# Grouped-query attention: VectorE empties two PSUM banks per instruction, chains of eight, last store on another queue

## The chip, the cores and the metric

The kernel runs on one core of a Trainium2 chip. The metric is device time in microseconds (us) of one execution; a median over runs is quoted. Ratios are computed as the mean time of one kernel's fast runs over that of the other's fast runs of the same rounds, with a 95% interval, so they are not quite the ratio of the medians. In the profiles PE is TensorE (PEld its weight loads), ACT is ScalarE, DVE is VectorE, POOL is GpSimd and SP is SyncE. Profiles are of single executions; the profiled span is about 1.7 us shorter than the device time.

## The reference, cut to what matters

```python
batch, n_q_heads, n_kv_heads, seq, head_dim = (8, 8, 2, 1024, 64)
scores = scale * np.matmul(q_group, k_group.transpose(0, 1, 3, 2))
attn = np.exp(scores - scores.max(-1, keepdims=True))
output = np.matmul(attn / attn.sum(-1, keepdims=True), v_group)
```

There are 64 heads. The kernel cuts each into two jobs of 512 queries, and each job into eight **cells** of 128 keys x 512 queries: 128 jobs, 1024 cells.

## The kernel before

PE computes the scores of a cell into one PSUM bank. Most cells go to ScalarE, which exponentiates two banks with one instruction. The others go to VectorE: it writes the scores as the bits of a power of two (evacuation), and a chain of four operations over a group of cells corrects them (named and, line, prod and add; line runs on POOL). PE then multiplies the result with the values ("output matmuls", 4 per cell), and VectorE normalises each job. A planner with a cost table decides at build time which cell goes where and in which order every engine runs; engines execute that order.

```python
A_CELLS, D_BANKS, O_BANKS = (2, 2), 2, 2     # ScalarE: 2 slots of 2 banks; VectorE: 2 single banks
GROUP, PARTS = 10, 2                         # cells per chain
...
    QK, PV, P1, NORM = 0.216, 0.1225, 0.603, 0.555
    EXP = (0.05, 0.4268)                     # planned cost of an exponential: fixed, per cell
...
    def exps(n, cells):                      # ScalarE
        act = nc.scalar.activation(
            out=pt[:, 0:m], in_=psum.pop(("A", n))[:, 0:m], func=AF.Exp, scale=scale
        )
...
    def exp_bits(cell, n, g, slot):          # VectorE, one bank
        nc.vector.tensor_scalar(
            out=groups[g][:, slot], in0=psum.pop(cell),
            scalar1=bits_scale, scalar2=bits_bias, op0=ALU.mult, op1=ALU.add,
        )
...
    def put_out(b, h, sides):
        nc.sync.dma_start(out=..., in_=stage[(b, h)][:, :, sides])
```

(cut at the marks and inside the calls)

The softmax here doesn't subtract the row's maximum and nothing guards it: scores larger than these inputs give would overflow.

## Time and profile before

| | before |
|---|---|
| device time, median of the first 3 runs | 385.65 us (385.5 to 385.9) |
| exponentials on ScalarE (2 cells each) | 404 |
| cells on VectorE | 216 |
| first exponential starts, last one ends | 7.40, 379.44 us |
| last normalisation ends, span ends | 380.59, 384.03 us |

The page's busy lines, its rows and the stages are shown in the prediction. One more view matters, and the prediction did not read it rightly: ScalarE's timeline in two nested windows (start us, length us, engine, line, operation, count).

```profile
157.58 1.94 ACT L477 ACTIVATE p_ring<-aps 128x1024 bf16<-128x1024 f32 x2
157.58 6.52 ACT L477 ACTIVATE p_ring<-aps 128x1024 bf16<-128x1024 f32 x7
```

A merged line ends where its last instruction ends. The second exponential of this stretch ends at 157.58 + 1.94 = 159.52, the seventh at 164.10: five intervals between **ends** take 4.58 us, 0.916 each. The trace's **starts** of the same instructions (158.50 to 163.015) take 4.517 us, 0.903 each. The recorded duration makes up the difference: 1.018, 1.032, 1.045, 1.058, 1.072, 1.085, some 13 ns more each time.

### The profile page before, as it was taken

How to read it: one execution, taken by the hardware profiler on the slowest of the kernel's cores; microseconds unless marked ns; L12 is line 12 of the kernel's file. 1: busy time of each engine (PE TensorE's matmuls, PEld its weight loads, DVE VectorE, ACT ScalarE, POOL GpSimd, SP SyncE). 2: the span in 40 equal slices, each digit the busy share in tenths (PEclk: the TensorE clock that was granted, in tenths of full speed). 3: DMA queues.
4: the chain of work that ended last, by engine and by line, in shares of the span. 5: the costliest groups of instructions: out<-in, count | busy, mean ns of one | idle time of the engine just before them, and what ended most of it. 6: DMA issues, size and time to landing. Idle time of an engine off the chain costs nothing.

```text
span 384.0 us, 12026 instructions
## 1 busy us (share of the span) xinstructions
PE 365.6 (95%) x5172; PEld 233.6 (61%) x5172; DVE 353.8 (92%) x548; ACT 374.6 (98%) x409; POOL 174.4 (45%) x147
## 2 busy tenths in 40 slices
PE   8879898999999999999999999999999999998995
PEld 7425464666666666666666666666666666564664
DVE  4779998999999999999999999999999999989982
ACT  5999999999999999999999999999999999999995
POOL 5584535718244371563718245271643627040420
PEclk9999999999999999999999999999999999999999
DMA  8988988697756848585676759468675765711213
GB/s 137 135 152 135 130 154 124 129 147 140 113 109 132 140 103 139 101 156 103 139 131 120 130 106 152 96 126 137 105 124 123 138 102 119 126 56 29 57 56 84
DMA packets 102485, 45.48 MB, mean 118 GB/s; under 512 B 63792, under 2 KB 100976, under 8 KB 101184
## 3 DMA queue, kind: packets, MB, share of 16 engines
q1 hardware_dynamic: 82096, 31.21, 36.1%
q0 software_dynamic: 19712, 13.18, 32.3%
q8 instruction: 40, 0.66, 0.7%
q10 hardware_dynamic: 624, 0.33, 0.3%
q14 instruction: 13, 0.11, 0.1%
HBM read 25.17 MB, written 27.00 MB: 136 GB/s over the span
## 4 chain that ended last, share of the span: by engine, by line
ACT 86%; PE 10%; DVE 2%; issue 1%
ACT p_ring L477 86%; PE aps L466 4%; PE ops L538 4%; PE ops L409 1%; PE dps L466 1%; DVE pd L527 1%; DVE ost L554 0%; DVE y L525 0%; DVE z L512 0%; DVE rec L551 0%; PE dps L382 0%; PE dps L428 0%; PE ops L428 0%; PE aps L382 0%; DVE blank L288 0%
## 5 line engine op out<-in xcount | busy, mean ns | idle before, releaser
L477 ACT ACTIVATE p_ring<-aps 128x1024 bf16<-128x1024 f32 x404 | 371.8, 1067 | 1.4 <-PE aps L466 1.2
L466 PE MATMUL aps<-qT,kset 128*128 128x512 bf16 x808 | 239.9, 378 | 13.0 <-ACT p_ring L477 12.4
L538 PEld LDWEIGHTS <-p_ring 128*128 128x128 bf16 x3232 | 140.1, 98 | 64.0
L538 PE MATMUL ops<-vset,p_ring 128*128 128x65 bf16 x3232 | 154.6, 194 | 0.0
L491 DVE TENSOR_SCALAR pd<-dps 128x512 uint16<-128x512 f32 x216 | 138.6, 683 | 7.0 <-PE dps L466 6.7
L516 POOL TENSOR_SCALAR y<-z 128x5120 f16<-128x5120 uint16 (+1 forms) x22 | 96.4, 4383 | 70.0 <-DVE rec L551 48.7
L466 PEld LDWEIGHTS <-kset 128*128 128x128 bf16 x1024 | 79.7, 97 | 56.4 <-issue 25.8
L323 POOL DMA_DIRECT2D scr_q<-in_q_dram x63 | 39.1, 621 | 83.5 <-PE dps L466 44.3
L466 PE MATMUL dps<-qT,kset 128*128 128x512 bf16 x216 | 76.4, 379 | 0.0
L525 DVE TENSOR_TENSOR y<-z,y 128x5120 f16<-128x5120 uint16 (+1 forms) x22 | 61.0, 2772 | 1.1 <-POOL y L516 1.1
L527 DVE TENSOR_TENSOR pd<-pd,y 128x5120 uint16<-128x5120 uint16 (+1 forms) x22 | 60.9, 2769 | 0.1
L554 DVE TENSOR_TENSOR ost<-ops,rec 128x256 f32<-128x256 f32 x128 | 54.3, 425 | 4.4
L538 PEld LDWEIGHTS <-pd 128*128 128x128 bf16 x864 | 42.8, 98 | 24.7 <-DVE ost L554 2.2
L538 PE MATMUL ops<-vset,pd 128*128 128x65 bf16 x864 | 52.2, 194 | 0.3
L512 DVE TENSOR_SCALAR z<-pd 128x5120 uint16<-128x5120 uint16 (+1 forms) x22 | 32.3, 1467 | 0.5
L551 DVE RECIPROCAL rec<-ops 128x4 f32<-128x4 f32 x128 | 22.6, 176 | 9.6 <-PE ops L538 8.2
L323 POOL DMA_DIRECT2D scr_k<-in_k_dram x15 | 9.8, 656 | 39.9 <-PE aps L466 33.0
L356 POOL DMA_DIRECT2D vset<-in_v_dram x32 | 24.9, 784 | 0.0
L409 PE MATMUL ops<-blank 128*128 128x128 bf16 x40 | 5.3, 313 | 1.1 <-DVE blank L288 1.1
L409 PEld LDWEIGHTS <-blank 128*128 128x128 bf16 x40 | 4.4, 149 | 1.1 <-DVE blank L288 1.1
L363 POOL DMA_DIRECT2D kset<-kset x6 | 4.1, 684 | 0.0
L420 ACT ACT_TABLE_LOAD x1 | 1.3, 1283 | 1.8 <-issue 1.8
(23 smaller groups left out, 10.2 us busy)
## 6 DMA issues: line engine op xcount, KB each, us to landing
out_dram<-ost SPq DMA_DIRECT2D x63, 256.0 KB, 2.9
scr_q<-in_q_dram POOLq DMA_DIRECT2D x63, 128.0 KB, 3.5
kset<-kT SPq DMA_DIRECT2D x60, 64.0 KB, 3.1
vset<-in_v_dram POOLq DMA_DIRECT2D x32, 64.0 KB, 3.9
scr_k<-in_k_dram POOLq DMA_DIRECT2D x15, 128.0 KB, 3.7
qT<-scr_q SPq DMA_TRANSPOSE x63, 3.5
kset<-kset POOLq DMA_DIRECT2D x6, 128.0 KB, 4.3
fq<-in_q_dram ACTq DMA_DIRECT2D x2, 128.0 KB, 3.3
```

What stands on the lines that cost most here:

```text
L323: dma = nc.gpsimd.dma_start(out=scr.rearrange("(p f) -> p f", f=1024), in_=src.rearrange("(p s) d -> p (s d)", s=1024 // D),)
L356: nc.gpsimd.dma_start(out=vsets[b % 2][:, g, two * NHC : (two + 1) * NHC, 0:D], in_=v[b, g].rearrange("(c p two) d -> two p c d", p=128, t ...
L466: last_score[0] = nc.tensor.matmul(dst, lhsT=ksets[b % 2][:, h // HPG, side, c * 128 : (c + 1) * 128], rhs=qT[(b, h)], start=True, stop=Tr ...
L477: act = nc.scalar.activation(out=pt[:, 0:m], in_=psum.pop(("A", n))[:, 0:m], func=AF.Exp, scale=scale)
L491: nc.vector.tensor_scalar(out=groups[g][:, slot], in0=psum.pop(cell), scalar1=bits_scale, scalar2=bits_bias, op0=ALU.mult, op1=ALU.add,)
L512: eng.tensor_scalar(out=z, in0=pd, scalar1=0x7F, scalar2=None, op0=ALU.bitwise_and)
L516: eng.tensor_scalar(out=y, in0=z, scalar1=CURVE_A / 128.0, scalar2=CURVE_B, op0=ALU.mult, op1=ALU.add,)
L525: eng.tensor_tensor(out=y, in0=z, in1=y, op=ALU.mult)
L527: eng.tensor_tensor(out=pd, in0=pd, in1=y, op=ALU.add)
L538: nc.tensor.matmul(ops_of[s][:, qs, :], lhsT=p_of[cell][:, qs * 128 : (qs + 1) * 128], rhs=vsets[b % 2][:, h // HPG, c, :], start=opens an ...
L551: nc.vector.reciprocal(out=rec, in_=o[:, :, D])
L554: nc.vector.tensor_tensor(out=stage[(b, h)][:, :, side, :], in0=o[:, :, 0:D], in1=rec.unsqueeze(2).to_broadcast([128, NQS, D]), op=ALU.mult,)
```

## The change

The intent: cheaper evacuations (one fixed cost for two banks), so that VectorE has slack; PSUM regrouped into three two-bank slots, two for ScalarE and one for VectorE; short chains at the start and at the end, where a late chain can't hide; the last store on a queue of its own.

```diff
-A_CELLS, D_BANKS, O_BANKS = (2, 2), 2, 2
-GROUP, PARTS = 10, 2
+SLOTS, A_SLOTS, D_SLOTS, O_BANKS = 3, (0, 1), (2,), 2
+GROUP, PARTS = 8, 2
...
-    LIVE_A, LIVE_D, PENDING, PER_JOB, LEAD, RAMP, AHEAD, FIRST_PV = 28, 5, 16, 2, 6, 6, 0.0, 2.0
-    AHEAD_D, EXTRA, LAST = 0, 0, 6
+    LIVE_A, LIVE_D, PENDING, PER_JOB, LEAD, RAMP, AHEAD, FIRST_PV = 28, 5, 12, 2, 4, 6, 0.06, 2.0
+    AHEAD_D = 0.03
+    FIRST_SIZES, FIRST_JOBS, FIRST_MORE = (2, 4, 6), 4, 2
+    LAST_SIZE, LAST_GROUPS, LAST_JOBS, LAST_MORE = 4, 8, 4, 0
...
-            out=groups[g][:, slot],
-            in0=psum.pop(cell),
+            out=groups[g][:, first : first + len(cells)],
+            in0=psum.pop(("D", slot))[:, 0 : len(cells)],
...
+                queue = nc.scalar if op[2] == len(jobs) - 1 else nc.sync
```

(cut: the planner's bookkeeping for pairs of cells, and the names of the PSUM pools)

More of the change, by code (lines that the diff above doesn't have):

```diff
@@ L26, in make_plan @@
 def make_plan(nj, nkc):
-    QK, PV, P1, NORM = 0.216, 0.1225, 0.603, 0.555
-    EXP = (0.05, 0.4268)
+    QK, PV, NORM = 0.216, 0.1225, 0.555
+    EXP, P1 = (0.05, 0.4268), (0.07, 0.533)
     FOUR, TWO, POOL_ONE = (0.09, 0.133), (0.05, 0.27), (0.25, 0.43)
@@ L44, in make_plan @@
     pe = act = dve = pool = two_end = 0.0
-    a_free, bank, obank_free = [0.0] * len(A_CELLS), [0.0] * D_BANKS, [0.0] * O_BANKS
+    free, obank_free = [0.0] * SLOTS, [0.0] * O_BANKS
     todo = [list(range(nkc)) for _ in range(nj)]
@@ L49, in make_plan @@
     open_jobs, next_job, rem, obank = [], 0, {}, {}
-    open_a = None
+    open_a = open_d = None
     ready, home, uses = {}, {}, {}
@@ L61, in loaded, with first_free, per_job, size @@
         return FIRST_LOAD + EACH_LOAD * (h - 1 if h < 4 else h)
-    def first_free(slots):
-        return min(range(len(slots)), key=lambda s: slots[s])
+    def first_free(times, among):
+        return min(among, key=lambda s: times[s])
+    def per_job(j):
+        if j < FIRST_JOBS:
+            return PER_JOB + FIRST_MORE
+        return PER_JOB + LAST_MORE * (j >= nj - LAST_JOBS)
+    def size(g):
+        if g < len(FIRST_SIZES):
+            return FIRST_SIZES[g]
+        return LAST_SIZE if job_d >= nj - LAST_GROUPS else GROUP
     while normed < nj:
@@ L73, in make_plan @@
         while job_d < nj and (
-            taken[job_d] >= PER_JOB + EXTRA * (job_d >= nj - LAST)
-            or not todo[job_d]
+            taken[job_d] >= per_job(job_d)
+            or len(todo[job_d]) < 2
         ):
@@ L82, in make_plan @@
             elif live["A"] < LIVE_A:
-                t = max(pe, min(a_free), loaded(job_a))
+                t = max(pe, min(free[s] for s in A_SLOTS), loaded(job_a))
             if t < INF:
                 best = min(best or (INF,), (t - AHEAD, 1, "qk", 0, t))
-        if job_d < nj and job_d <= job_a + lead + 1 and pending < PENDING:
+        if open_d is not None:
+            t = max(pe, open_d["t"])
+            best = min(best or (INF,), (t - AHEAD_D, 2, "qk", 1, t))
+        elif job_d < nj and job_d <= job_a + lead + 1 and pending < PENDING:
             if cur or live["D"] < LIVE_D:
-                t = max(pe, min(bank), loaded(job_d))
+                t = max(pe, min(free[s] for s in D_SLOTS), loaded(job_d))
                 if t < INF:
@@ L110, in make_plan @@
             best = min(best or (INF,), (at, 2 + i, "chain", i))
-        if cur and job_d >= nj and not p1q:
+        if cur and job_d >= nj and not p1q and open_d is None:
             best = min(best or (INF,), (dve, 9, "flush", 0))
@@ L116, in make_plan @@
             pe = t + QK
-            j = job_d if arg else job_a
-            cell = j * nkc + todo[j].pop(0)
             if not arg:
+                cell = job_a * nkc + todo[job_a].pop(0)
                 if open_a is None:
-                    slot = first_free(a_free)
+                    slot = first_free(free, A_SLOTS)
                     a_id += 1
                     live["A"] += 1
-                    open_a = {"slot": slot, "t": a_free[slot], "cells": []}
-                    a_free[slot] = INF
+                    open_a = {"slot": slot, "t": free[slot], "cells": []}
+                    free[slot] = INF
                 o = open_a
@@ L129, in make_plan @@
                 home[cell] = ("A", a_id)
-                if len(o["cells"]) == A_CELLS[o["slot"]] or not any(todo[job_a:]):
+                if len(o["cells"]) == 2 or not any(todo[job_a:]):
                     act = max(act, pe + FROM_PE)
@@ L133, in make_plan @@
                     act += EXP[0] + EXP[1] * len(o["cells"])
-                    a_free[o["slot"]] = act + FROM_ACT
+                    free[o["slot"]] = act + FROM_ACT
                     uses[("A", a_id)] = len(o["cells"])
@@ L139, in make_plan @@
             else:
-                taken[j] += 1
-                k = first_free(bank)
-                bank[k] = INF
-                pending += 1
-                ops.append((t, "qk", cell, "D", k, 0, 0))
-                p1q.append((pe + FROM_PE, cell, k))
+                if open_d is None:
+                    slot = first_free(free, D_SLOTS)
+                    open_d = {"slot": slot, "t": free[slot], "n": 0}
+                    open_d["cells"] = [job_d * nkc + todo[job_d].pop(0) for _ in range(2)]
+                    free[slot] = INF
+                    taken[job_d] += 2
+                    pending += 2
+                o = open_d
+                cell = o["cells"][o["n"]]
+                ops.append((t, "qk", cell, "D", cell, o["slot"], o["n"]))
+                o["n"] += 1
+                if o["n"] == 2:
+                    p1q.append((pe + FROM_PE, tuple(o["cells"]), o["slot"]))
+                    open_d = None
         elif kind == "open":
-            o = first_free(obank_free)
+            o = first_free(obank_free, range(O_BANKS))
             obank[arg] = o
@@ L174, in make_plan @@
         elif kind == "p1":
-            _, cell, k = p1q.pop(0)
+            _, cells, slot = p1q.pop(0)
             if not cur:
@@ L178, in make_plan @@
                 live["D"] += 1
-            ops.append((t, "p1", cell, k, d_id, len(cur)))
-            dve = t + P1
-            bank[k] = dve + FROM_DVE
-            cur.append(cell)
-            home[cell] = ("D", d_id)
-            if len(cur) == GROUP:
+            ops.append((t, "p1", cells, slot, d_id, len(cur)))
+            dve = t + P1[0] + P1[1] * len(cells)
+            free[slot] = dve + FROM_DVE
+            for x in cells:
+                cur.append(x)
+                home[x] = ("D", d_id)
+            if len(cur) >= size(d_id):
                 chainq.append((dve, d_id, cur, 0))
@@ L282, in psum_pools @@
         ]
-    apools, dbanks, obanks = psum_pools("aps", 2), psum_pools("dps", 2), psum_pools("ops", 2)
+    slots, obanks = psum_pools("sps", SLOTS), psum_pools("ops", O_BANKS)
     p_ring = const_pool.tile([128, P_TILES, 2, QBS], BF16)
@@ L372, in first_loads @@
         hk = first_pool.tile([128, NHC, 3, D], BF16, name="hk")
-        tk = [
-            dbanks[0].tile([128, HALF], BF16, name="dps0"),
-            apools[1].tile([128, HALF], BF16, name="aps1"),
+        spare = [
+            slots[n].tile([128, 2, 2 * QBS], BF16, name=f"sps{n}")[:, 0, :HALF]
+            for n in range(SLOTS)
         ]
+        tk = [spare[2], spare[1]]
         lo, hi = slice(0, D), slice(D, 2 * D)
@@ L412, in first_loads @@
         hq = first_pool.tile([128, NHC, 2 * D], BF16, name="hq")
-        tq = [
-            dbanks[1].tile([128, HALF], BF16, name="dps1"),
-            obanks[0].tile([128, HALF], BF16, name="ops0"),
-        ]
+        tq = [spare[0], obanks[0].tile([128, HALF], BF16, name="ops0")]
         qT[(0, 0)] = qT_pool.tile([128, HALF], BF16, name="qT")
@@ L459, in score @@
         c = cell % NKC
+        if col == 0:
+            psum[kind, slot] = slots[slot].tile([128, 2, QBS], FP32, name=f"sps{slot}")
+        dst = psum[kind, slot][:, col, :]
         if kind == "A":
-            if col == 0:
-                psum[("A", n)] = apools[slot].tile([128, 2, QBS], FP32, name=f"aps{slot}")
-            dst = psum[("A", n)][:, col, :]
-        else:
-            dst = psum[cell] = dbanks[n].tile([128, QBS], FP32, name=f"dps{n}")
+            psum["exp", n] = psum[kind, slot]
         last_score[0] = nc.tensor.matmul(
@@ L477, in exps @@
         act = nc.scalar.activation(
-            out=pt[:, 0:m], in_=psum.pop(("A", n))[:, 0:m], func=AF.Exp, scale=scale
+            out=pt[:, 0:m], in_=psum.pop(("exp", n))[:, 0:m], func=AF.Exp, scale=scale
         )
@@ L486, in exps, with exp_bits @@
             p_of[cell] = pt[:, col, :]
-    def exp_bits(cell, n, g, slot):
-        if slot == 0:
+    def exp_bits(cells, slot, g, first):
+        if first == 0:
             groups[g] = pd_pool.tile([128, GROUP, QBS], U16, name="pd")
         nc.vector.tensor_scalar(
-            out=groups[g][:, slot],
-            in0=psum.pop(cell),
+            out=groups[g][:, first : first + len(cells)],
+            in0=psum.pop(("D", slot))[:, 0 : len(cells)],
             scalar1=bits_scale,
@@ L498, in exp_bits @@
         )
-        p_of[cell] = groups[g][:, slot].bitcast(BF16)
+        for n, cell in enumerate(cells):
+            p_of[cell] = groups[g][:, first + n].bitcast(BF16)
     def exp_curve(g, m, step):
@@ L559, in normalise, with put_out @@
         )
-    def put_out(b, h, sides):
+    def put_out(b, h, sides, queue):
         rows = "(s p two) d -> p s two d"
-        nc.sync.dma_start(
+        queue.dma_start(
             out=out[b, h].rearrange(rows, p=128, two=2)[:, :, sides],
@@ L576 @@
             if op[2] >= len(jobs) - 2:
-                at(op[0] + 0.01, put_out, b, h, slice(side, side + 1))
+                queue = nc.scalar if op[2] == len(jobs) - 1 else nc.sync
+                at(op[0] + 0.01, put_out, b, h, slice(side, side + 1), queue)
             elif ended.setdefault(op[2] // 2, op[2]) != op[2]:
-                at(op[0] + 1.5, put_out, b, h, slice(0, 2))
+                at(op[0] + 1.5, put_out, b, h, slice(0, 2), nc.sync)
         at(op[0], run[op[1]], *op[2:])
```

## The prediction

> **What bounds the kernel now.** I read the page first, then windows, then the chain of waits and PE's timeline near the end. The page's part 1, its chain by engine, and its rows (line, engine, operation, shapes, count | busy us, mean ns | idle before, releaser):
>
> ```profile
> PE 365.6 (95%) x5172; PEld 233.6 (61%) x5172; DVE 353.8 (92%) x548; ACT 374.6 (98%) x409; POOL 174.4 (45%) x147
> ACT 86%; PE 10%; DVE 2%; issue 1%
> L477 ACT ACTIVATE p_ring<-aps 128x1024 bf16<-128x1024 f32 x404 | 371.8, 1067 | 1.4 <-PE aps L466 1.2
> L466 PE MATMUL aps<-qT,kset 128*128 128x512 bf16 x808 | 239.9, 378 | 13.0 <-ACT p_ring L477 12.4
> L491 DVE TENSOR_SCALAR pd<-dps 128x512 uint16<-128x512 f32 x216 | 138.6, 683 | 7.0 <-PE dps L466 6.7
> ```
>
> ScalarE is busy 98% and carries 86% of the chain. Its 404 exponentials of two cells each do 808 of the 1024 score cells; VectorE does the other 216, one cell (one PSUM bank) at a time. Per stage (columns: stretch, length, then busy time of PE, PEld, DVE, ACT, POOL, then granted clock, DMA share, GB/s):
>
> ```profile
> 0.00:10.00 10.00, 8.69 (x72) 6.98 (x73) 4.61 (x13) 5.32 (x8) 5.12 (x15) 1.00 0.77 131
> 60.00:340.00 280.00, 273.69 (x3979) 176.35 (x3975) 273.17 (x420) 279.95 (x306) 129.47 (x103) 1.00 0.71 123
> 340.00:380.00 40.00, 38.07 (x618) 25.29 (x616) 32.79 (x53) 39.34 (x43) 10.98 (x3) 1.00 0.17 48
> ```
>
> In the long middle ScalarE never shows a gap, VectorE is busy 97.6% (273.17 of 280) and PE nearly as much. But "busy" hides small waits on ScalarE: one exponential is recorded as 1.067 us, yet the next starts before its end. The start times in the trace tell the rest: 403 intervals from 7.40 to 378.35 us, shortest 0.903 us, 193 of them under 0.905, mean 0.9205. The excess over 403 x 0.903 = 363.9 is **7.0 us**. In 123 intervals the exponential starts within 45 ns of the modelled end of the second score matmul that feeds it: these PE released, and they hold 5.0 of the 7.0 us. PE's timeline shows why (start, us, engine, line, operation):
>
> ```profile
> 374.00 0.59 PE L466 MATMUL aps<-qT,kset 128*128 128x512 bf16 x2
> 374.44 0.65 PE L538 MATMUL ops<-vset,p_ring 128*128 128x65 bf16 x16
> 374.93 0.59 PE L466 MATMUL aps<-qT,kset 128*128 128x512 bf16 x2
> ```
>
> From one pair of scores for ScalarE to the next, PE spends 0.93 us when 16 output matmuls (4 cells) stand between; that is more than 0.903. The chain of waits splits this step (start, us, what):
>
> ```profile
> 374.17 0.43 PE aps L466 x2
> 374.60 0.49 PE ops L538 x16
> ```
>
> So ScalarE is the bound, and PE's in-order program adds to it whenever one step carries more than 0.903 us of work. Only two PSUM slots feed ScalarE, so PE cannot run ahead to hide it.
>
> **What the Trainium skill says.** "Perfetto Trace Analysis", section "Identifying the Most-Contended Engine", takes occupancy as the measure for ScalarE and VectorE; the 98% agrees, with the correction above that a 98% engine still loses 7 us to late inputs. "VectorE: DVE Perf Modes", section on the TRN2 errata, gives a PSUM to SBUF operation 120 + FD cycles at 0.96 GHz: 658 ns for 512 elements, where the trace has 683. For 1024 it gives 1.19 us; adding 512 elements at 1.04 ns to the traced 683 gives 1.22. "DMA: Bandwidth & Descriptors", section "Issuing engines are not separate DMA queues", says that issuing from another engine saves only the sequencer's time to issue; see the last store below.
>
> **The change part by part.**
>
> *One VectorE instruction for two banks.* In the instruction order of the two built programs 216 evacuations of 512 become 107 of 1024. Three of the old ones in a row take 1.94 us merged, so they follow each other at about (1.94 - 0.68) / 2 = 0.63, at best 0.60 us (two take 1.28). New: estimated 1.22 - 0.08 of overlap = 1.13 us. 216 x 0.60 = 129.6; 107 x 1.13 = 120.9: VectorE saves 8.7 us.
>
> *Chains.* 22 chains (21 of ten cells, one of six) become 30 (23 of eight, two of six, four of four, one of two). From the two forms of each row (5120 and 3072 elements: 1491 and 954 ns, 2820 and 1759, 2817 and 1749) the constant part of an operation is about 0.15 us recorded. Three VectorE operations x 8 more chains x at most 0.15 = +3.6 us; two cells fewer give back 1.3. VectorE ends with some 6.4 us less, near 347 us. POOL's line gets 8 more instructions of a constant of some 0.2 us; at 45% that costs nothing. Since VectorE is off the chain, its saving is worth nothing by itself.
>
> *Cells do not move.* VectorE's share goes from 216 to 214, so ScalarE does 405 exponentials, not 404: **+0.90 us** on the bound.
>
> *PE's order.* The planner is changed (score pairs for VectorE stand together, ScalarE's pairs get 0.06 us of precedence). I counted in the built order what stands between one ScalarE pair and the next. Pair 0.43, VectorE score 0.215, output matmuls 0.03 each:
>
> - 16 outputs: 0.92, over by 0.018: 131 steps before, 177 after
> - one VectorE score and 12 outputs: 1.015, over by 0.11: 26 before, 8 after
> - two and 4: 0.98, over by 0.08: 33 before, 15 after
> - two and 8: over by 0.20: 2 before, none after
> - 20 outputs: over by 0.14: 4 before, none after
>
> Sums: before 2.4 + 2.9 + 2.6 + 0.4 + 0.6 = 8.9 us, after 3.2 + 0.9 + 1.2 = 5.3 us. Light steps in between absorb part of it: of the 8.9 the trace shows 5.0 (0.56). With the same share the new order costs 3.0 us: **-2.0 us**. The gain is that a lone VectorE score with 8 outputs (92 steps) or 12 gives way to whole pairs with none (10 to 73 steps, 0.86 us, which fits).
>
> *Ends.* The first chain is two cells, and the last ones four, so outputs at the ends wait less for VectorE. The first exponential still waits for the same loads, at 7.40 us: nothing. After the last exponential (ends 379.44) the old kernel needs 1.15 us for the last outputs and the normalisation and 3.4 us for the last store and the end: that stays. The issue of the last store was not held up on its old queue: VectorE ends at 380.59, the issue starts at 380.62. It landed 2.5 us later, behind a 256 KB store issued 0.6 us ahead. In the new order the last two normalisations stand further apart, so the last store shares the DMA engines less: about **-0.3 us**, not because of the queue.
>
> Sum: +0.90 - 2.0 - 0.3 = -1.4 us, 384.2. The share of 0.56 is probably lower with many small overruns of 0.018 and few large ones, because a light step absorbs a small one whole; I lower the value to **383.9 us**.
>
> **Rivals.**
>
> 1. *The single VectorE slot stalls PE.* Before, two banks were refilled one at a time; now both belong to one instruction, and PE can't put in a new pair until it is read. A cycle takes some 0.6 (two scores) + 1.2 + waits of 0.1 = 1.9 us; 107 pairs in 350 us come every 3.3 us, so on average it fits, but a chain operation of eight cells takes 8/10 of 2.8 = 2.2 us, and a pair that comes just before it would hold the slot for over 4 us. PE is in order: a wait there delays ScalarE's next pair directly. For it: nothing on PE waits for VectorE before (0.0 idle at its VectorE scores), so there is no measure. Against: VectorE gets slack, 97.6% to some 95%, and the planner places a pair only when it expects the slot to be free. If every tenth pair stalled by 0.4 us: +4 us, 387.5.
> 2. *Nothing but the extra exponential.* If the waits are a matter of how tightly two slots can turn round, not of PE's order, the 7.0 us stay and the time is 385.65 + 0.9 - 0.3 = 386.2. Against it: intervals of 0.92 us (130 of them) and of 0.98 to 1.01 are just what the step sums above give.
> 3. *VectorE was the true limit, and its saving counts.* At 97.6% it paces the output banks and chains. Then the remaining 2 us of excess vanish as well, and the time is near 382. Against: only 2.2 us of weight-load idle is put down to VectorE's normalisation, 1.9 to its chains.
>
> **Range and chances.** With all 7.0 us of excess gone the time would be 385.65 + 0.9 - 7.0 - 0.3 = 379.25, 1.7% under the old: over 2% faster is out of reach unless the lead-in shrinks. Rival 1 has to cost over 9 us for 2% slower. Range 381.9 to 386.2. Faster 0.01, within 2% 0.96, slower 0.03.
>
> **What would show it.** Right: 405 exponentials; evacuations near 1.2 us; VectorE busy near 347 us; VectorE's share of the middle near 95%; mean exponential interval 0.914 to 0.917; no PE row that waits for VectorE over 1 us in total; last store lands 2.0 to 2.3 us after its issue. Wrong: PE scores waiting for VectorE's evacuation by several us (rival 1), an unchanged mean interval of 0.920 (rival 2), or a first exponential later than 7.4 us because the start now uses ScalarE's first slot for a transpose.

## The result, and the profile after

Over 6 runs each, the changed kernel took 384.98 us (384.9 to 385.48), the kernel before 385.77: ratio **0.9984** (0.9971 to 0.9997). In a later set of rounds it was 385.11 against 385.61, 0.9989 (0.9977 to 1.0001). So it is some 0.1 to 0.2% faster, 0.4 to 0.6 us by these ratios (the second interval just takes in 1), where I had predicted 1.75 us (383.9).

The page after, part 1, the chain by engine, and the rows that answer to those shown before. The trace of this execution lacks 92 matmul records (5080 of 5172), so PE's busy times are a little low:

```profile
PE 364.8 (95%) x5080; PEld 235.4 (61%) x5172; DVE 349.3 (91%) x463; ACT 374.4 (98%) x410; POOL 174.1 (45%) x155
...
ACT 91%; PE 5%; DVE 2%; POOL 1%; issue 0%
...
L497 ACT ACTIVATE p_ring<-sps 128x1024 bf16<-128x1024 f32 x405 | 371.7, 1111 | 1.2 <-PE sps L486 1.1
L486 PE MATMUL sps<-qT,kset 128*128 128x512 bf16 x932 | 262.1, 378 | 8.7 <-ACT p_ring L497 6.3
...
L511 DVE TENSOR_SCALAR pd<-sps 128x1024 uint16<-128x1024 f32 x107 | 130.7, 1221 | 11.9 <-PE sps L486 10.7
```

VectorE works less and ScalarE's share of the chain grew from 86% to 91%. The tell-tale is the mean duration of an exponential: 1111 ns, up from 1067, with no more time in total. The stages after:

```profile
0.00:10.00 10.00, 8.56 (x72) 6.86 (x74) 4.54 (x12) 5.76 (x9) 5.67 (x16) 1.00 0.80 137
...
60.00:340.00 280.00, 272.26 (x3874) 176.28 (x3944) 265.82 (x346) 279.71 (x306) 130.89 (x104) 1.00 0.70 121
340.00:380.00 40.00, 37.65 (x584) 25.31 (x591) 34.05 (x53) 39.09 (x43) 8.78 (x4) 1.00 0.21 58
```

VectorE fell from 97.6% to 94.9% of the middle, as expected, and ScalarE did the same 306 exponentials in the same 280 us as before. The chain of waits (the profile's walk back from the instruction that ended last; not to be confused with VectorE's chains) shows the pace: it names ScalarE for stretches of 26 exponentials (start, us, what). Before:

```profile
152.93 23.86 ACT p_ring L477 x26
176.86 23.80 ACT p_ring L477 x26
```

After:

```profile
151.98 23.78 ACT p_ring L497 x26
175.81 23.85 ACT p_ring L497 x26
```

From one stretch to the next it is 23.93 us before and 23.83 after: 0.9204 and 0.9165 us per exponential. PE's lateness did fall, but there were only 0.004 us per exponential to win here.

From here on I use ends of exponentials. In every profile the median interval between ends is 0.916 to 0.917 us; I call **excess** the time from the first to the last end beyond 0.9165 us per interval.

| profile | exponentials | first start | first to last end | excess | intervals over 0.93 | last end to last normalisation | last store, issue to landing |
|---|---|---|---|---|---|---|---|
| before | 404 | 7.40 | 371.01 | 1.66 | 25 | 1.16 | 2.50 |
| after | 405 | 6.96 | 371.10 | 0.84 | 4 | 1.15 | 2.01 |

(landing: when SP's wait for the store ends)

The profiled spans differ by 0.83 us (384.03, 383.21): start -0.44, one exponential +0.92, excess -0.82, last store -0.50, rest +0.01. The start turned out to be chance (below), so what the change brings is about -0.4 us.

### The profile page after: what moved, and what is told of

Same layout as the page of the kernel before. It is cut to its first block, busy times and chain, and to the rows that moved or that the text cites. A ratio compares the mean times of both kernels' runs of the same rounds, so it can differ in the third digit from the quotient of the medians.

```text
span 383.2 us, 11861 instructions
## 1 busy us (share of the span) xinstructions
PE 364.8 (95%) x5080; PEld 235.4 (61%) x5172; DVE 349.3 (91%) x463; ACT 374.4 (98%) x410; POOL 174.1 (45%) x155
## 4 chain that ended last, share of the span: by engine, by line
ACT 91%; PE 5%; DVE 2%; POOL 1%; issue 0%
ACT p_ring L497 91%; PE sps L486 2%; PE ops L433 1%; PE ops L559 1%; POOL y L537 1%; DVE y L546 1%; DVE pd L548 1%; POOL scr_q L346 0%; DVE ost L575 0%; PE sps L406 0%; DVE rec L572 0%; PE ops L449 0%; PE sps L449 0%; POOL vset L379 0%; DVE blank L311 0%
## 5 line engine op out<-in xcount | busy, mean ns | idle before, releaser
L497 ACT ACTIVATE p_ring<-sps 128x1024 bf16<-128x1024 f32 x405 | 371.7, 1111 | 1.2 <-PE sps L486 1.1
L486 PE MATMUL sps<-qT,kset 128*128 128x512 bf16 x932 | 262.1, 378 | 8.7 <-ACT p_ring L497 6.3
L559 PEld LDWEIGHTS <-p_ring 128*128 128x128 bf16 x3240 | 133.7, 97 | 57.0 <-ACT p_ring L497 0.8
L559 PE MATMUL ops<-vset,p_ring 128*128 128x65 bf16 x3240 | 145.9, 194 | 4.1 <-ACT p_ring L497 0.5
L511 DVE TENSOR_SCALAR pd<-sps 128x1024 uint16<-128x1024 f32 x107 | 130.7, 1221 | 11.9 <-PE sps L486 10.7
L537 POOL TENSOR_SCALAR y<-z 128x4096 f16<-128x4096 uint16 (+3 forms) x30 | 97.4, 3248 | 49.2 <-DVE z L533 48.9
L546 DVE TENSOR_TENSOR y<-z,y 128x4096 f16<-128x4096 uint16 (+3 forms) x30 | 61.7, 2056 | 2.8 <-POOL y L537 2.2
L548 DVE TENSOR_TENSOR pd<-pd,y 128x4096 uint16<-128x4096 uint16 (+3 forms) x30 | 61.6, 2054 | 0.3
L559 PE MATMUL ops<-vset,pd 128*128 128x65 bf16 x856 | 40.4, 194 | 1.0 <-DVE pd L548 0.5
L533 DVE TENSOR_SCALAR z<-pd 128x4096 uint16<-128x4096 uint16 (+3 forms) x30 | 33.2, 1109 | 0.8
```

The costliest lines, as they stand in the source:

```text
L486: last_score[0] = nc.tensor.matmul(dst, lhsT=ksets[b % 2][:, h // HPG, side, c * 128 : (c + 1) * 128], rhs=qT[(b, h)], start=True, stop=Tr ...
L497: act = nc.scalar.activation(out=pt[:, 0:m], in_=psum.pop(("exp", n))[:, 0:m], func=AF.Exp, scale=scale)
L511: nc.vector.tensor_scalar(out=groups[g][:, first : first + len(cells)], in0=psum.pop(("D", slot))[:, 0 : len(cells)], scalar1=bits_scale, ...
L533: eng.tensor_scalar(out=z, in0=pd, scalar1=0x7F, scalar2=None, op0=ALU.bitwise_and)
L537: eng.tensor_scalar(out=y, in0=z, scalar1=CURVE_A / 128.0, scalar2=CURVE_B, op0=ALU.mult, op1=ALU.add,)
L546: eng.tensor_tensor(out=y, in0=z, in1=y, op=ALU.mult)
```

## The experiments

"Theory" is that ScalarE's own pace is 0.9165 us and that the time is the number of exponentials at that pace, plus a small excess, plus the two ends.

**1. PE with slack.** Some output steps left out of the kernel before, with a wrong result (the matmul count falls from 5172 to 3640):

```diff
+        if c % 2 and not opens and not closes:
+            p_of.pop(cell)
+            return
```

> The kernel before with about three of eight output steps left out (wrong result on purpose), so that PE has slack and cannot be late for ScalarE. Theory (ScalarE's own pace is 0.9165 us per exponential, measured from end to end; start-to-start intervals of 0.903 only mean that an instruction is recorded earlier and longer): intervals between ends settle at 0.916 to 0.917, the recorded duration saturates near 1.15 us, first to last end takes 403 x 0.9165 = 369.4 us instead of 371.0, and the time falls by about 1.6 us, to some 384.1. Rival (my prediction: pace 0.903, the rest is PE): starts follow at 0.903, first to last start takes 364 us, the time falls by 5 to 7 us, to 379 to 381.

Measured: 384.07 us, ratio 0.996 (0.9947 to 0.9974). Relieved of 30% of its matmuls, PE lets ScalarE run no faster than this (chain of waits):

```profile
152.65 23.79 ACT p_ring L477 x26
176.48 23.79 ACT p_ring L477 x26
```

23.83 us per 26, 0.9165 each, again. The recorded durations climb to 1.15 us and stop there (median 1.130), and starts are then 0.917 apart too. The rival, on which the prediction stood, is refuted: a start that follows 0.903 us after the one before is not a pace that ScalarE can keep. After a late start the durations fall back (to 1.02 to 1.09) and climb again, and while they climb the starts are closer than the ends. A further rival is that the turn-round of the two slots sets this pace: in this run PE's scores began within 60 ns of the end of the exponential two before in 354 of 402 cases. But 169 exponentials began over 60 ns after the modelled end of their scores, so that PE and the slot no longer held them, and their ends too followed 0.917 us after the one before. And 187 exponentials began within 45 ns of their scores, more than the 123 of the kernel before, although PE had slack: that sign does not tell that PE is late. Of the 25 intervals over 0.93 us, 5 remain. First to last end took 370.8 us, not 369.4, because one early interval lost 1.11 us; the waits name its cause:

```profile
PE dps L466 <- DMA kset<-kset: 1.2, 1, 1.2
```

This execution began at 6.55 us instead of 7.40, and PE then waited for a copy of keys: an early start was given back. It is therefore partly luck that the time met the theory's 384.1: against the profile before, the start came 0.86 us earlier and the last store landed 0.29 us sooner, which the wait of 1.11 us nearly cancels.

**2 and 3. The queue of the last store.** The changed kernel with it back on SP's queue, and the kernel before with it on ScalarE's:

```diff
-                queue = nc.scalar if op[2] == len(jobs) - 1 else nc.sync
+                queue = nc.sync
```
```diff
-        nc.sync.dma_start(
+        (queue or nc.sync).dma_start(
...
+                   nc.scalar if op[2] == len(jobs) - 1 else nc.sync)
```

> The changed kernel with the very last store back on SP's queue. Theory (the gain at the end, 0.50 us between issue and landing, comes from the distance to the store before it, not from the queue): the last store still lands about 2.0 us after its issue, and the time stays within 0.1 us of the changed kernel's 384.98. Rival (the queue gives it): the store lands after about 2.5 us and the time is 0.4 to 0.5 us longer, 385.4.

> The kernel before with only its very last store moved to ScalarE's queue. Theory (distance counts, not queue): the store still lands about 2.5 us after its issue because a 256 KB store was issued 0.6 us ahead of it, time within 0.1 us of before, 385.7. Rival (the queue gives it): landing in 2.0 us, time 385.2.

Measured: 385.37 us (0.9990, interval 0.9976 to 1.0004) and 385.37 us (0.9998, 0.9985 to 1.001). The times alone do not tell the theories apart, as 0.4 us lies within both intervals. The traces do: the last store landed 1.98 us after its issue in the first, 2.50 us in the second, each as in the kernel with the same plan (2.01 and 2.50) and not as in the kernel with the same queue. In the plan before, a 256 KB store was issued 0.6 us ahead of the last one; in the plan after, 1.9 us ahead. Profiles of later experiments lie between, each with a 256 KB store ahead: 2.21 us for 0.88 us ahead, 2.16 for 0.93, 2.11 for 0.99. The distance counts. The change of queue brought nothing that these runs show.

**4. One bank per instruction in the new plan.** Same slots, same order, two instructions for each pair:

```diff
-        nc.vector.tensor_scalar(
-            out=groups[g][:, first : first + len(cells)],
-            in0=psum.pop(("D", slot))[:, 0 : len(cells)],
+        src = psum.pop(("D", slot))
+        for n in range(len(cells)):
+            nc.vector.tensor_scalar(
+                out=groups[g][:, first + n],
+                in0=src[:, n],
```

> The changed kernel, same plan and slots, but each evacuation of two banks split again into two VectorE instructions of 512. Theory (VectorE is off the path, its 8 us saved buy nothing by themselves): VectorE's busy time rises by some 7 us to 356, ScalarE's ends still follow at 0.9165, time within 0.5 us of 384.98. Rival (the merged instruction itself brings the gain, because the single slot comes free sooner): PE waits for the slot, ScalarE's excess over 0.9165 per exponential grows from 0.8 us to several, time 386 or more.

Measured: 385.97 us, 1.0009 (0.9995 to 1.0023), 1.0 us above the changed kernel's 384.98 (of another round; 0.6 above experiment 2 of the same round): my theory, that VectorE's saving buys nothing, missed, and the rival came nearer. VectorE was busy 354.5 us. The excess was 2.50 us, nearly all of it in 16 intervals; 0.62 of it is an early wait for the copy of keys as in experiment 1 (this execution began at 6.49 us), the remaining 1.9 compare with 0.84. The largest interval after that, 0.48 us near 252 us, is PE's output matmuls waiting for the last operation of a chain (chain of waits):

```profile
249.24 2.21 DVE pd L550
251.45 0.05 issue
251.50 0.30 PE ops L561 x4
...
252.26 1.94 ACT p_ring L497 x2
```

The scores for ScalarE stand behind the delayed outputs in PE's order. But the changed kernel loses 0.39 us at the same exponential, by the same wait:

```profile
248.48 2.21 DVE pd L548
...
250.73 0.30 PE ops L559 x4
```

So this chain makes 0.08 us of the difference. Most of the rest is the single slot. One case (timeline):

```profile
185.39 1.28 DVE L513 TENSOR_SCALAR pd<-sps 128x512 uint16<-128x512 f32 x2
...
186.21 0.53 PE L561 MATMUL ops<-vset,p_ring 128*128 128x65 bf16 x12
...
186.72 1.02 PE L486 MATMUL sps<-qT,kset 128*128 128x512 bf16 x4
```

The twelve outputs follow each other 0.03 us apart, so PE could begin VectorE's next pair of scores at 186.58. It begins at 186.72, 53 ns after the second evacuation has ended, and ScalarE's pair stands behind it. Counted in this way from the trace and the built order, 31 pairs of VectorE's scores waited for the slot, 2.85 us of PE's time in all, and 13 of the 16 late intervals, with 1.10 us, follow such a pair within 1.3 us. In the changed kernel it is 8 pairs, 0.58 us, and 2 of its 4 late intervals, with 0.14 us. The lists of waits do not show this: an output matmul is recorded as 0.19 us, so a short wait leaves no idle time between records. So the merged instruction is worth some 0.6 to 1 us in this plan, and mainly because the single slot comes free sooner, as the rival had it. Whether through the evacuation itself (1.22 us against 1.28) or because VectorE, with less to do, comes to it sooner was not separated.

**5. The changed kernel again**, as the yardstick for the next runs.

> The changed kernel once more, as the yardstick of this round. Theory: 405 exponentials, first to last end 371.1 us with 4 intervals over 0.93 us, last store landing in 2.0 us; the first exponential starts anywhere from 6.5 to 7.5 us, by when PE's clock comes up in that execution, so its start says nothing about the change. Time 384.8 to 385.4.

Measured: 385.11 us, ratio 0.9989; 371.10 us from first to last end, excess 0.83, 4 intervals over 0.93, landing 2.01 us: all as in the first profile. The first exponential began at 7.26 us instead of 6.96.

**6. Without the precedence for ScalarE's score pairs.**

```diff
-... FIRST_PV = 28, 5, 12, 2, 4, 6, 0.06, 2.0
-    AHEAD_D = 0.03
+... FIRST_PV = 28, 5, 12, 2, 4, 6, 0.0, 2.0
+    AHEAD_D = 0.0
```

> The changed kernel with the planner's precedence for ScalarE's score pairs (0.06 and 0.03 us) set to zero. Its plan has 404 exponentials, one fewer. Theory (ScalarE's pace 0.9165 plus what PE is late): the missing exponential gives -0.92 us, and if the precedence is what keeps PE on time, the excess over 0.9165 grows from 0.8 to 2 us or more and takes that back; at least ten intervals over 0.93 us. Rival (the two-bank slots alone keep PE on time): excess stays at 0.8 us, first to last end 370.2 us.

Measured: 384.92 us, 0.9986 (0.9974 to 0.9998). First to last end 370.21 us with an excess of 0.86: the rival held, in total. The lateness is spread otherwise (22 small intervals instead of 4), but not larger. By the prediction's way of counting, the steps of this order are over by 9.7 us in sum (151 steps with 16 outputs, 12 with one score and 12, 47 with two and 4, 2 with two and 8, 11 with 20), more than the 8.9 before; yet the excess is half of that before. So this sum does not foretell the lateness. The exponential that the plan saves is lost at the end, where the last normalisation comes 1.84 us after the last exponential instead of 1.15, and the last store lands 0.15 us later.

**7. Without short chains.**

```diff
-    FIRST_SIZES, FIRST_JOBS, FIRST_MORE = (2, 4, 6), 4, 2
-    LAST_SIZE, LAST_GROUPS, LAST_JOBS, LAST_MORE = 4, 8, 4, 0
+    FIRST_SIZES, FIRST_JOBS, FIRST_MORE = (), 4, 2
+    LAST_SIZE, LAST_GROUPS, LAST_JOBS, LAST_MORE = 8, 8, 4, 0
```

> The changed kernel with chains of eight throughout, none short at the ends; its plan has 406 exponentials, one more. Theory: first to last end grows by 0.92 us for the exponential, and the end after the last exponential stays at 1.15 us to the last normalisation plus the store; time longer by 0.9 to 1.3 us than the changed kernel of the same round, the short chains being worth one exponential and not a wait. Rival (short chains remove waits at the ends): excess in the first 60 and the last 40 us grows by over 1 us on top.

Measured: 387.38 us, 1.0047 (1.0035 to 1.0059), 2.3 us above the changed kernel of the round, about twice what I expected. The extra exponential is one part (0.92). (The start is not: this execution began at 6.42 us and lost 0.73 us again to the copy of keys.) The end is another: the chain of waits ends with

```profile
378.51 0.43 PE sps L486 x2
378.94 2.60 PE ops L559 x84
381.54 0.02 issue
```

84 output matmuls, those of 21 cells, still had to be done after the last scores; the last normalisation came 2.09 us after the last exponential (1.15 in the changed kernel), and a large store was again close ahead of the last one (landing 2.52 us). So the short chains at the end are worth 0.94 us of normalisation and 0.5 us of store. The exponential can be due to those at the start as well, which this run also drops.

**8. A plan with the measured pace and 402 exponentials.** If the time is a count of exponentials, fewer must help:

```diff
-    EXP, P1 = (0.05, 0.4268), (0.07, 0.533)
+    EXP, P1 = (0.05, 0.4333), (0.07, 0.533)
-... FIRST_PV = 28, 5, 12, 2, 4, 6, 0.06, 2.0      (AHEAD_D 0.03, GROUP 8)
+... FIRST_PV = 28, 5, 16, 2, 6, 10, 0.1, 2.0      (AHEAD_D 0.05, GROUP 10)
-    LAST_SIZE, LAST_GROUPS, LAST_JOBS, LAST_MORE = 4, 8, 4, 0
+    LAST_SIZE, LAST_GROUPS, LAST_JOBS, LAST_MORE = 6, 12, 4, 2
```

(cut: FIRST_JOBS from 4 to 6)

> The changed kernel with its planner told ScalarE's measured pace (0.9166 for two cells in place of 0.9036) and other limits, so that VectorE takes 220 cells and ScalarE 402 exponentials, three fewer. Theory (time is the number of exponentials at 0.9165 plus a small excess): first to last end 401 x 0.9165 + 0.8 = 368.3 us, 2.7 us shorter than the changed kernel; time about 382.3. Rival (VectorE with its 6 cells more becomes the bound, or PE waits for the single slot): the excess grows to 3 us or more and the time is no better than 385.

Measured: 385.22 us, 0.9997 (0.9985 to 1.0009): no better. The rival's number held, an excess of 3.41 us. Nearly half of it, 1.42, is one interval near 373 us (chain of waits):

```profile
367.99 1.68 DVE y L546
369.67 0.02 issue
369.69 3.34 DVE pd L548
373.03 0.04 issue
373.08 0.66 PE ops L559 x16
373.74 0.45 PE sps L486 x2
```

PE's outputs waited for a chain that came late, and ScalarE's scores stood behind them. The slot takes another part: counted as in experiment 4, 48 pairs of VectorE's scores waited for it, 5.2 us of PE's time, and 22 of the 27 late intervals, with 1.1 us, follow such a pair.

**9 to 11. Fewer exponentials with chains on time.** Two plans with 403 exponentials, chains of ten in the middle and four at the end, in which the planner also reckons with longer delays after ScalarE, VectorE and POOL; and one told the pace without these delays. Its edit changes two more limits (PER_JOB from 2 to 4, RAMP from 6 to 8).

```diff
-    EXP, P1 = (0.05, 0.4268), (0.07, 0.533)
+    EXP, P1 = (0.05, 0.4333), (0.07, 0.533)
-    ... FROM_ACT, FROM_DVE, FROM_POOL = 0.21, 0.16, 0.165, 0.10, 0.15
+    ... FROM_ACT, FROM_DVE, FROM_POOL = 0.21, 0.16, 0.2, 0.15, 0.4      (first two only)
-... FIRST_PV = 28, 5, 12, 2, 4, 6, 0.06, 2.0                             (GROUP 8)
+... FIRST_PV = 28, 5, 16, 2, 6, 8, 0.05, 2.0                             (first; GROUP 10)
+... FIRST_PV = 28, 5, 16, 2, 5, 10, 0.06, 2.0                            (second; GROUP 10)
+... FIRST_PV = 28, 5, 12, 4, 4, 8, 0.06, 2.0                             (third; GROUP 8)
```

(cut: in the first two also AHEAD_D and the sizes of the first and last chains)

> The changed kernel with the planner told the measured pace of ScalarE and longer delays from VectorE and POOL, chains of ten in the middle, four at the end: 403 exponentials, two fewer. Theory: what spoiled the plan with 402 exponentials was one late chain near the end (one interval of 2.33 us), so with short last chains and true delays the excess comes down to 1 us or less; first to last end 402 x 0.9165 + 1 = 369.4 us, 1.7 us less than the changed kernel's 371.1; time about 383.4. Rival: with more cells VectorE is late everywhere, excess 2.5 us or more, time 385.

> As the run before, with another set of limits (also 403 exponentials). Theory: same, about 383.4. If one of the two holds and the other does not, the placing of the chains decides, not the number of cells.

> The changed kernel with the planner told ScalarE's measured pace only, chains of eight and short ends as in the change, 403 exponentials. Theory: 402 x 0.9165 + 0.8 to 1.5 = 369.2 to 369.9 us from first to last end; time about 383.5. Rival: excess 2.5 us or more, time 385.

Measured: **383.2** (0.9935, 0.9922 to 0.9948), **383.46** (0.9939, 0.9927 to 0.995) and 387.42 us (1.0044, 1.0028 to 1.006). The first two beat both kernels and came out within 0.2 us of what the count gives: first to last end 369.73 and 369.95 us, excess 1.29 and 1.51. The third has the same number of exponentials and an excess of 6.32 us. (Its six runs alternate between 386.6 to 386.8 and 388.0 to 388.4 us, and the profile is of the longer kind; why was not found.) Its waits:

```profile
PEld L559 <- DVE pd L548: 8.8, 16, 2.2
...
ACT p_ring L497 <- PE sps L486: 4.1, 6, 1.8
```

The same two waits in the best plan:

```profile
PEld L559 <- DVE pd L548: 2.5, 4, 0.8
...
ACT p_ring L497 <- PE sps L486: 1.6, 3, 0.7
```

Not VectorE's load decides: it was busy 350.9 us in the best of these and 354.3 in the third, and in the middle (60 to 340 us) 267.3 and 267.1. What differs is how long PE waits: for chains at its outputs, as these lists show, and, which they don't show, for the single slot: 33 pairs, 3.6 us, against 6 pairs, 0.5 us, in the best plan (counted as in experiment 4). The largest late interval of the third, 1.89 us, stands behind a chain that ended at 356.0 us; late intervals with 1.5 us follow pairs that waited for the slot. Which of the altered limits kept both waits short in the good plans was not separated.

**The start.** Over 13 profiles the first exponential began between 6.42 and 7.47 us. In the six that began after 7 us, PE's 128-column matmuls followed each other 107 ns apart right up to the scores; in the seven that began earlier they came down to 56 ns first, at moments from 3.8 to 5.9 us. "TensorE: Matmul & The Clock Gate", part 1 on the clock gate, says that the window which decides this is free-running, so that the point of change varies with where the first matmul lands in it; these profiles agree in kind, though their spread is wider than the 0.5 us to either side that the page gives. The -0.44 us between the two first profiles is of this kind: the changed kernel's own profiles began at 6.96 and at 7.26 us. And the earliest starts lose part of it again to the copy of keys. A systematic difference of some 0.1 us at the start is not excluded by so few profiles.

## Why the prediction was wrong

The bound, the direction and three of the terms held; **the size of the gain from PE's order did not**, and it was most of the predicted gain.

- *ScalarE is the bound, +0.90 us for one exponential more.* Right: 0.92.
- *"shortest 0.903 us ... The excess over 403 x 0.903 = 363.9 is 7.0 us", of which PE holds 5.0.* This is the step that failed. The floor was read from start-to-start intervals. ScalarE's pace is 0.9165 us, as ends show in each profile and as experiment 1 shows with slack on PE. 403 x 0.0135 = 5.4 of the 7.0 us are ScalarE's own work; 1.66 (measured from ends) were lateness. That exponentials started within 45 ns of PE's scores was true and misleading: when the engine is a little behind in its cycle, a late start costs nothing at the end (in experiment 1, starts 0.98 us apart were often followed by ends 0.917 apart).
- *"Sums: before 8.9, after 5.3 us ... with the same share the new order costs 3.0 us: -2.0 us".* The count of PE's steps was right, and so was the sign: the excess halved, 1.66 to 0.84. With the true floor a step of 16 outputs (0.92) is hardly late at all. In place of -2.0 stands **-0.82**. That nearly cancels the extra exponential. And the share of 0.56 does not carry over to another order: that of experiment 6 sums to 9.7 us and has an excess of 0.86. So that the sign came out as predicted does not confirm the count. The mean interval named as a sign of being right, 0.914 to 0.917, came out as 0.918.
- *A further -0.3 us by judgement*, because small overruns would be absorbed: nothing was left for it.
- *Last store -0.3 us, from distance and not from the queue.* Right in kind (experiments 2 and 3), 0.50 in size.
- *VectorE's saving "is worth nothing by itself".* Wrong by some 0.6 to 1 us (experiment 4): off the chain on average, it is on it wherever PE waits for the single slot or for a late chain. Its size was roughly right: busy 349.3 us (predicted 347), 94.9% of the middle (95%).
- *Rival 1, the single slot stalls PE.* Happened, but small: 8 pairs waited 0.58 us in all, and 0.14 us of the excess follows them; in the plan of experiment 8 some 1.1 us do. The reading that nothing on PE waited for VectorE before was wrong: counted as in experiment 4, 17 of VectorE's scores waited for their bank there, 1.7 us. *Rival 2* (386.2) was nearer than I thought: most of the 7.0 us does stay, but as ScalarE's own work and not as the turn-round of two slots (experiment 1).
- *"The first exponential still waits for the same loads, at 7.40 us".* Misread: the chain of waits before has PE's warm-up and transposing matmuls back to back from 1.06 to 6.79 us, and no load. The start moves with PE's clock (above).

The sum with measured terms is 0.92 - 0.82 - 0.50 = -0.40 us; the two sets of rounds give -0.4 and -0.6. Not settled: whether the paired slots or another limit of the plan made PE less late (the precedence alone did not, experiment 6).

## What to carry to other kernels

Before crediting an engine's lateness to its supplier, find the engine's true pace between ends over a long undisturbed stretch, or from a run in which the supplier has slack; the shortest start-to-start interval is not it. Once ScalarE was at its pace here, little but fewer exponentials was left to win: moving four cells to VectorE and keeping the chains on time shortened the stretch from first to last end by 1.4 us (371.10 to 369.73), which the change itself had left as it was. And in an in-order program a helper engine that is off the path on average still sets the time wherever its result, or the buffer that it empties, is due; and PE's waits that are shorter than a recorded matmul can be missing from the list of waits, so they have to be counted from the start times.

## What the Trainium skill lacked or had wrong

- "Perfetto Trace Analysis", section "Optimizing Scalar/DVE Operations", gives per-instruction overheads of about 51 ns for ScalarE and 125 ns for VectorE on PSUM. Back-to-back exponentials of 1024 elements here take 0.9165 us between ends; 1024 elements at 1.2 GHz (this clock and the next from the table in "VectorE: DVE Perf Modes", section on the TRN2 errata) are 0.853 us, so the overhead is an estimated 63 ns. Back-to-back evacuations of 512 elements follow each other 0.597 us apart in the trace; 512 elements at 0.96 GHz are 0.533 us, so the overhead is an estimated 64 ns, half of the page's.
- The same page's timeline of a ScalarE instruction does not say that recorded starts can run closer together (0.903 us) than the engine's pace (0.9165) while the recorded duration climbs from 1.02 to 1.15 us, 13 ns at a time.
- "VectorE: DVE Perf Modes", section on the TRN2 errata: 120 + FD cycles give an estimated 1.19 us for the two-bank evacuation; recorded 1.221 us, 2.5% more. Close.
- No page that I read gives the time to landing of a store behind another one: 128 KB landed 2.0 us after its issue with a 256 KB store 1.9 us ahead, 2.5 us with one 0.6 us ahead, on either queue.
